# HGRN decays grown in place by doubling blocks, in a two-layer FoX/HGRN2 trunk on one core

## The chip, the cores and the metric

The kernel runs on one core of a Trainium2 chip. TensorE (PE) multiplies matrices into the PSUM banks, VectorE (DVE) and ScalarE (ACT) work element by element, GpSimd (POOL) does a few small things, and SyncE (SP) issues nearly all loads. The metric is device time in microseconds (us), the median of the runs.

## The reference, cut to what matters

The model has two layers, each with a SwiGLU half-step, a mixer and another SwiGLU half-step, over 256 positions of 1024 channels. The mixer of the first layer is an attention (FoX); that of the second, at about 70% of the span, is HGRN2, and the change lies there:

```
f = lb + (1.0 - lb) * jax.nn.sigmoid(proj[..., D:2 * D])
k = 1.0 - f
# per head (8 of them, 128 channels each), with G the running sum of log f over positions:
A[t, s] = sum over channels of  q[t] * k[s] * exp(G[t] - G[s])      for s <= t
o[t]    = sum over s of  A[t, s] * v[s]
```

exp(G[t] - G[s]) is the product of f over the positions s+1 to t. The kernel never forms it for each pair. It splits the pairs by levels: for the block size b = 64, 32, ..., 1 the pairs whose s lies in the left half and t in the right half of the same stretch of 2b positions. With the middle m of that stretch the decay is (product from s+1 to m) times (product from m to t), so that one matrix product of a decayed k and a decayed q gives a level.

## The kernel before

**Stream.** All products with weights are done as three matmuls (`mm3`, lines 745 to 747; for v in `v_token`, lines 896 to 898), on weights that come by DMA into 8 `raw` tiles and are split by ACT (`wh`, a cast, line 385) and DVE (`wl`, line 386) into a high and a low part, two blocks of weights ahead (`SPLIT_AHEAD`; `wh` and `wl` have three buffers each). Each `mm3` is a tick. Side work is written as Python generators that are advanced after so many ticks (`HG_LAG`), so that its instructions stand between those of the stream; the tile framework then fixes the order on each engine. Every engine works through its own order, one instruction after the other.

**The HGRN stage.** `hgrn` runs the blocks hgf (4, giving f and kk = 1 - f), then hgq, hgv and hgg in the order of `HG_ORDER`, then hgo, the output projection. Each half block of hgq gives the q of one head and starts its generator `hgrn_head`; up to three run at once, and of one E buffer (two exist, for even and odd heads) a head waits until the head two before it is through with its levels. ACT takes Ln of all f at once after the last Sigmoid (line 1093).

**A head.** (1) PE turns log f of its 256 positions (`plf`, line 1128, two transposes), and ACT and DVE split it into two parts (`lt`, lines 1130 and 1131). (2) PE multiplies it with a constant matrix `tmat` of prefix sums, four matmuls of 512 columns (line 1140) and four of 256 (line 1146) into the bank `pd`, which gives the log decays of the levels. (3) ACT takes Exp of them (lines 1141 and 1148; line 1150 copies f by Exp as well), and DVE multiplies them on k and q (lines 1154 to 1176). (4) PE makes `pc`, the products of the diagonal (line 1182) and of the two halves of the sequence (line 1184), and `pA`, those of the seven levels (line 1192); DVE puts them in place in `at` (line 1195, copy under a mask). (5) PE multiplies `at` by v (`pho`, lines 1203 to 1205), ACT and POOL normalise it, and PE turns it back (`hpr`, line 1218). The products of (4) and (5) are on fp32, of which the trace shows two passes for each matmul.

**Constants.** `tmat` is loaded by POOL in two parts (`tm`, lines 616 and 619) at about 64 us; the attention uses 128 of its columns.

Of the kernel before, what the change touches and what calls it, by code (L numbers as in the profile page):

```python
# [11 lines left out]
F32 = mybir.dt.float32  # L12
F32R = mybir.dt.float32r
# [6 lines left out]
P = 128  # L20
# [11 lines left out]
TM = (len(LEV) - 1) * P  # L32
# [10 lines left out]
HG_LAG = (4, 7, 14, 12, 12)  # L43
# [16 lines left out]
def shape_constants():  # L60
# [4 lines left out]
    rcross = (i[:, None] >= i[None, :]).astype(np.float32)  # L65
    tl, tr = [], []
    masks = np.zeros((P, len(LEV), P), np.int32)
    for li, b in enumerate(LEV):
        T = np.zeros((P, P), np.float32)
        for t in range(P):  # L70
            g0 = t // (2 * b) * (2 * b)
            mid = g0 + b
            if t >= mid:
                T[mid:t + 1, t] = 1
            else:
                T[t + 1:mid, t] = 1
# [13 lines left out]
    tmat = np.concatenate([lcross] + tl[:-2] + [rcross] + tr[:-2], axis=1)  # L90
    return (np.ascontiguousarray(consts), np.ascontiguousarray(tmat),
# [15 lines left out]
class Trunk:  # L107
# [29 lines left out]
    # ------------------------------------------------- interleaving of side work  # L137
# [44 lines left out]
    # ---------------------------------------------------------------- stream  # L182
# [235 lines left out]
    # ------------------------------------------------------------------- ada  # L418
# [89 lines left out]
    # ----------------------------------------------------------------- setup  # L508
    def setup(self):
# [41 lines left out]
        self.tm = cp.tile([P, TM], F32R, name="tm")  # L551
# [64 lines left out]
        nc.gpsimd.dma_start(self.tm, a["tmat"][:, :TM])  # L616
        tm1 = self.wk.tile([P, D], F32R, tag="wide", name="tm1", bufs=1)
        nc.vector.tensor_copy(tm1[:, 0:1], self.hbuf[0][:, KC - 1, 0:1])
        nc.gpsimd.dma_start(tm1[:, :TM], a["tmat"][:, TM:])
        self.hg_tm = [self.tm, tm1]  # L620
# [44 lines left out]
    # ------------------------------------------------------------------ norm  # L665
# [74 lines left out]
    # -------------------------------------------------------------- products  # L740
# [101 lines left out]
    # ------------------------------------------------------------------- ffn  # L842
# [64 lines left out]
    # ------------------------------------------------------------------- fox  # L907
    def fox(self, n):
# [53 lines left out]
        def cum_tail():  # L962
            yield CUM_LAG[0]
            pz = self.bank("zt")
            nc.tensor.transpose(pz[:, :M], z[:M, P:], self.ident[:M, :M])
            zt = self.w("zt")
            nc.scalar.copy(zt[:, :M], pz[:, :M])
            yield CUM_LAG[1]
            pz = self.bank("cum")
            nc.tensor.matmul(pz[:M, :P], zt[:, :M], self.tm[:, :P].bitcast(F32), start=True, stop=True)  # L970
            nc.vector.scalar_tensor_tensor(cum[:M, P:], pz[:M, :P], cum[:M, P - 1:P], z[:M, P:], ALU.add, ALU.add)
# [85 lines left out]
    # ------------------------------------------------------------------ hgrn  # L1057
    def hgrn(self, n):
# [10 lines left out]
        parts = [reg(4)[:, :D], reg(4)[:, D:]]  # L1069
        parts += [big[:, 10240:], wk.tile([P, D], F32, tag="adaacc", name="E_adaacc", bufs=1)]  # L1070
        parts = [t.rearrange("p (l c) -> p l c", c=P) for t in parts]
        self.hE = [parts[:2], parts[2:]]
        ox = self.ubuf
        self.hspare = wk.tile([P, S], F32, tag="adatr", name="hspare", bufs=1).rearrange("p (i c) -> p i c", i=2)

        def use_f(b, ps, sw=None):
            for c in range(2):
                h = 2 * b + c
                pc = ps[c]
                if sw is None:  # L1080
                    sg = nc.scalar.activation(f[:, h, :], pc, AF.Sigmoid)
                else:
                    sg = nc.scalar.activation(f[:, h, :], pc, AF.Sigmoid, bias=sw[:, c:c + 1])
                self.last_sig = sg.ins
# [38 lines left out]
    def hgrn_head(self, h, qs, kk, lf, v):  # L1123
        nc, wk = self.nc, self.wk
        q, k = qs[:, h, :], kk[:, h, :]
        pt = self.bank("plf")
        for t in range(2):
            nc.tensor.transpose(pt[:, t * P:(t + 1) * P], lf[:, h, t * P:(t + 1) * P], self.ident)
        lt = wk.tile([P, 512], F32R, tag="mx", name="lt", bufs=6).rearrange("p (j s) -> p j s", j=2)
        nc.scalar.copy(lt[:, 0], pt[:, :S])  # L1130
        nc.vector.tensor_tensor(lt[:, 1], pt[:, :S], lt[:, 0].bitcast(F32), ALU.subtract)
        yield HG_LAG[0]
        while h >= 2 and h - 2 not in self.e_done:
            yield E_POLL
        E = self.hE[h % 2]
        E0, E1 = E
        for t in range(2):
            pd = self.bank("pd")
            for j in range(2):
                nc.tensor.matmul(pd, lt[:, j, t * P:(t + 1) * P], self.hg_tm[t][:, :512], start=(j == 0), stop=(j == 1))  # L1140
            nc.scalar.activation(E0[:, t::2], pd.rearrange("p (l c) -> p l c", c=P), AF.Exp)
            yield HG_LAG[1]
        pd = self.bank("pd")
        for t in range(2):
            for j in range(2):
                nc.tensor.matmul(pd[:, t * S:(t + 1) * S], lt[:, j, t * P:(t + 1) * P], self.hg_tm[t][:, 512:TM],
                                 start=(t == 0 and j == 0), stop=(j == 1), skip_group_check=True)
        nc.scalar.activation(E1[:, :4].rearrange("p (l t) c -> p t l c", t=2),
                             pd.rearrange("p (t l c) -> p t l c", t=2, c=P), AF.Exp)
        nc.scalar.activation(E1[:, 4:8:2], lf[:, h, :].rearrange("p (t c) -> p t c", t=2), AF.Exp)  # L1150
        yield HG_LAG[1]
        lev = [E0[:, 2 * li:2 * li + 2] for li in range(1, 4)] + [E1[:, 2 * li:2 * li + 2] for li in range(4)]
        lev = [x.rearrange("p t c -> p (t c)") for x in lev]
        nc.vector.tensor_tensor(E0[:, 0, :], E0[:, 0, :], k[:, :P], ALU.mult)
        nc.vector.tensor_tensor(E0[:, 1, :], E0[:, 1, :], q[:, P:], ALU.mult)
        free = self.hspare[:, h % 2, :]
        ab = []
        for x, b in zip(lev[:-2], LEV):
            nc.vector.tensor_tensor(pick(free, *pair(b, b)), pick(x, *pair(b, P)), pick(k, *pair(b, P + b)), ALU.mult)
            nc.vector.tensor_tensor(pick(x[:, P:], *pair(b, b)), pick(x[:, b:], *pair(b, P)),  # L1160
                                    pick(q[:, b:], *pair(b, P - b)), ALU.mult)
            ab.append((free, x[:, P:]))
            free = x[:, :P]
# [129 lines left out]
```

## Time and profile before

| | us |
|---|---|
| median of 3 runs (1119.0 to 1120.95) | 1120.65 |
| span of the profiled execution | 1119.9 |
| PE busy | 1095.8 |
| DVE busy | 847.6 |
| ACT busy | 590.3 |
| POOL busy | 24.0 |

A busy PE is not a PE at its peak, since matmuls overlap; what a matmul costs the engine is the time to the next one, and it is read from the chain of waits. The HGRN stage with its heads lies between 793 and 903 us.

### The profile page before, as it was taken

To read this page: it belongs to the slowest core of one execution; us is meant where nothing else is said; L and a number is where in the kernel's file an instruction comes from. 1 tells how busy PE (TensorE), PEld (TensorE's weight loads), DVE (VectorE), ACT (ScalarE), POOL (GpSimd) and SP (SyncE) were. 2 spreads that over 40 slices of the span, in tenths; PEclk is the share of its full clock that TensorE was granted. 3 is DMA by queue.
4 is the path that set the end of the run, shared out by engine and by line. 5 is a ranking of instruction groups with operands and counts; after the bars stand their busy time and mean duration, and the time that the engine had idled before them with its cause. 6 is when DMAs were issued, how large, how long until landed. Compare 5 with 4: busy or idle time off the path is not lost.

```text
span 1119.9 us, 22226 instructions
## 1 busy us (share of the span) xinstructions
PE 1095.8 (98%) x8915; PEld 1066.5 (95%) x8915; DVE 847.6 (76%) x1519; ACT 590.3 (53%) x1041; POOL 24.0 (2%) x47
## 2 busy tenths in 40 slices
PE   5999999999999999999999999999999999999997
PEld 5999999988989999999999999999899999999997
DVE  6988778577995997788689888768878979555542
ACT  5464444476864754444454444346776656444443
POOL 0000000010000000000000000000000000000000
PEclk8999999999999999999999999999999999999999
DMA  9999999659783599999759999985634247665530
GB/s 287 336 336 327 327 316 289 193 192 330 249 272 102 151 278 304 308 319 320 209 175 298 295 320 338 298 250 171 186 126 136 81 133 200 190 183 172 177 110 38
DMA packets 304852, 260.97 MB, mean 233 GB/s; under 512 B 9541, under 2 KB 281389, under 8 KB 304749
## 3 DMA queue, kind: packets, MB, share of 16 engines
q1 hardware_dynamic: 304172, 257.79, 76.3%
q8 instruction: 70, 1.15, 0.4%
q0 software_dynamic: 432, 1.25, 0.3%
q10 hardware_dynamic: 144, 0.52, 0.1%
q14 instruction: 34, 0.27, 0.1%
HBM read 258.47 MB, written 1.05 MB: 232 GB/s over the span
## 4 chain that ended last, share of the span: by engine, by line
PE 77%; issue 18%; ACT 2%; DMA 1%; POOL 1%; SPq 0%; DVE 0%; POOLq 0%; DVEq 0%; ACTq 0%
PE pf L746 17%; PE pf L745 17%; PE pf L747 16%; PE pd L745 6%; PE pd L746 6%; PE pd L747 6%; PE pA L1192 1%; PE pv L898 1%; PE pv L897 1%; PE pv L896 1%; PE adaps L479 1%; PE sc L1015 1%; PE pd L1140 1%; DMA raw<-in_ffn_w_up_dram 1%; ACT wh L385 1%
## 5 line engine op out<-in xcount | busy, mean ns | idle before, releaser
L746 PE MATMUL pf<-hbuf,wh 128*128 128x256 f32 (+1 forms) x1920 | 542.4, 284 | 0.9 <-DVE hbuf L602 0.9
L747 PE MATMUL pf<-hbuf,wl 128*128 128x256 f32 (+1 forms) x1920 | 541.5, 283 | 0.0
L745 PE MATMUL pf<-hbuf,wh 128*128 128x256 f32 (+1 forms) x1920 | 538.1, 284 | 0.6 <-ACT hbuf L601 0.6
L385 ACT CAST wh<-raw 128x1024 fp32r<-128x1024 f32 x338 | 341.2, 1027 | 372.1 <-PE pf L746 207.8
L386 DVE TENSOR_TENSOR wl<-raw,wh 128x1024 fp32r<-128x1024 f32 x338 | 400.2, 1195 | 158.9 <-ACT wh L385 157.7
L745 PEld LDWEIGHTS pf<-hbuf,wh 128*128 128x128 f32 x1920 | 362.7, 191 | 5.1 <-issue 4.0
L746 PEld LDWEIGHTS pf<-hbuf,wh 128*128 128x128 f32 x1920 | 363.7, 189 | 1.4 <-DVE hbuf L602 1.1
L747 PEld LDWEIGHTS pf<-hbuf,wl 128*128 128x128 f32 x1920 | 363.3, 189 | 0.8 <-issue 0.8
L745 PE MATMUL pd<-gx,wh 128*128 128x256 f32 x704 | 198.4, 282 | 0.0
L746 PE MATMUL pd<-gx,wh 128*128 128x256 f32 x704 | 197.4, 280 | 0.0
L747 PE MATMUL pd<-gx,wl 128*128 128x256 f32 x704 | 197.4, 280 | 0.0
L426 DVE SCALAR_TENSOR_TENSOR adaacc<-raw,cond,adaacc 128x1024 f32<-128x1024 f32 x112 | 143.0, 1277 | 0.6
L745 PEld LDWEIGHTS pd<-gx,wh 128*128 128x128 f32 x704 | 132.6, 188 | 2.5 <-issue 2.5
L746 PEld LDWEIGHTS pd<-gx,wh 128*128 128x128 f32 x704 | 132.6, 188 | 0.0
L747 PEld LDWEIGHTS pd<-gx,wl 128*128 128x128 f32 x704 | 132.6, 188 | 0.0
L811 ACT CAST gx<-g 128x256 fp32r<-128x256 f32 x88 | 35.6, 406 | 25.9 <-DVE g L853 17.6
L813 DVE TENSOR_TENSOR gx<-g,gx 128x256 fp32r<-128x256 f32 x88 | 36.8, 420 | 0.3
L424 DVE TENSOR_SCALAR adaacc<-raw,cond 128x1024 f32<-128x1024 f32 x16 | 12.1, 756 | 25.2 <-PE adaps L479 25.2
L853 DVE TENSOR_TENSOR g<-sa,pf 128x256 f32<-128x256 f32 x73 | 30.1, 415 | 0.6 <-ACT sa L852 0.2
L818 DVE SCALAR_TENSOR_TENSOR x<-pd,mod,x 128x256 f32<-128x256 f32 x32 | 14.3, 480 | 21.1 <-PE pd L747 21.1
L852 ACT ACTIVATE sa<-pf 128x256 f32<-128x256 f32 x73 | 27.4, 377 | 0.0
L374 ACT CAST wh<-raw 128x896 fp32r<-128x896 f32 x16 | 15.0, 936 | 23.0 <-DMA raw<-in_ffn_w_up_dram 23.0
(246 smaller groups left out, 894.9 us busy)
## 6 DMA issues: line engine op xcount, KB each, us to landing
raw<-in_ffn_w_up_dram SPq DMA_DIRECT2D x162, 512.0 KB, 5.8
raw<-in_ada_w_dram SPq DMA_DIRECT2D x128, 512.0 KB, 6.1
raw<-in_ffn_w_down_dram SPq DMA_DIRECT2D x76, 512.0 KB, 5.5
raw<-in_fox_w_in_dram SPq DMA_DIRECT2D x32, 512.0 KB, 4.9
raw<-in_hgrn_w_in_dram SPq DMA_DIRECT2D x32, 512.0 KB, 4.6
raw<-in_ada_w_dram SPq DMA_DIRECT2D x32, 256.0 KB, 6.5
raw<-in_ffn_w_up_dram SPq DMA_DIRECT2D x16, 448.0 KB, 6.3
raw<-in_fox_w_out_dram SPq DMA_DIRECT2D x8, 512.0 KB, 5.7
```

The source lines that it names most:

```text
L374: nc.scalar.copy(wh[:, k, cs], raw)
L385: nc.scalar.copy(wh[:, ks, cs], raw)
L386: nc.vector.tensor_tensor(wl[:, ks, cs], raw, wh[:, ks, cs].bitcast(F32), ALU.subtract)
L426: nc.vector.scalar_tensor_tensor(self.ada_acc, raw, self.cond[:, k:k + 1], self.ada_acc, ALU.mult, ALU.add)
L745: nc.tensor.matmul(ps, wh, hx[:, :n], start=first, stop=False, skip_group_check=True)
L746: nc.tensor.matmul(ps, wh, hx[:, lo:lo + n], start=False, stop=False, skip_group_check=True)
L747: nc.tensor.matmul(ps, wl, hx[:, :n], start=False, stop=last, skip_group_check=True)
L811: nc.scalar.copy(dst[:, :S], v)
L813: nc.vector.tensor_tensor(dst[:, lo:lo + S], v, dst[:, :S].bitcast(F32), ALU.subtract)
L818: nc.vector.scalar_tensor_tensor(self.x[:, m, :], ps, gate[:, m:m + 1], self.x[:, m, :], ALU.mult, ALU.add)
L852: nc.scalar.activation(sa, ps[0], AF.Silu)
L853: nc.vector.tensor_tensor(g, sa, ps[1], ALU.mult)
```

## The change

The logarithm, the prefix sums, the Exp and the transposes go. The decays are products of f that grow with b. Before the levels, `totals` multiplies neighbouring f for all heads at once: `tot2` holds the products of pairs, `tot4` of fours, and `tots` those of 8, 16, 32 and 64. In a head q is first multiplied by f. Then at each level, b = 1 first, ACT copies the left halves of k and the right halves of q into two packed slots (`snap`), the operands of that level's product; after that DVE multiplies in place those parts of q and k that lie beyond the next middle by the total of their neighbour block (`grow`), and b doubles. The levels 1 to 8 are multiplied in one bank, 16 to 64 in a second, with the product of the two halves, which has left `pc`. The E buffers become slots; `tmat` shrinks from 1536 to 128 columns; `HG_LAG` changes.

```diff
-HG_LAG = (4, 7, 14, 12, 12)
+HG_LAG = (4, 4, 5, 12, 12)
...
-        nc.gpsimd.dma_start(self.tm, a["tmat"][:, :TM])
-        nc.gpsimd.dma_start(tm1[:, :TM], a["tmat"][:, TM:])
+        nc.gpsimd.dma_start(self.tm, a["tmat"])
...
-        with self.tc.issue_after(self.last_sig):
-            for b in range(2):
-                nc.scalar.activation(f[:, 4 * b:4 * b + 4, :], f[:, 4 * b:4 * b + 4, :], AF.Ln)
+        self.totals(f)
...
+    def totals(self, f):
+        halve = lambda o, x: nc.vector.tensor_tensor(o, x[:, 0::2], x[:, 1::2], ALU.mult)
+        halve(self.tot2, flat)
+        for i in range(2):
+            halve(self.tot4[i], self.tot2[:, i * 512:(i + 1) * 512])
+            halve(self.tots[:, i * P:(i + 1) * P], self.tot4[i])
+        for n in (256, 128, 64):
+            halve(self.tots[:, o + n:o + n + n // 2], self.tots[:, o:o + n])
+
+    def grow(self, x, t, b, left):
+        m = P // b
+        if left:
+            v, w = pick(x, *pair(b, P + b)), pick(t[:, 1:], [m - 1, 2], [2, m // 2], [0, b])
+        else:
+            v, w = pick(x[:, b:], *pair(b, P - b)), pick(t, [m + 1, 2], [2, m // 2], [0, b])
+        self.nc.vector.tensor_tensor(v, v, w, ALU.mult)
...
-        for t in range(2):
-            nc.tensor.transpose(pt[:, t * P:(t + 1) * P], lf[:, h, t * P:(t + 1) * P], self.ident)
-        nc.scalar.copy(lt[:, 0], pt[:, :S])
-        nc.vector.tensor_tensor(lt[:, 1], pt[:, :S], lt[:, 0].bitcast(F32), ALU.subtract)
...
-                nc.tensor.matmul(pd, lt[:, j, t * P:(t + 1) * P], self.hg_tm[t][:, :512], start=(j == 0), stop=(j == 1))
-            nc.scalar.activation(E0[:, t::2], pd.rearrange("p (l c) -> p l c", c=P), AF.Exp)
...
+        nc.vector.tensor_tensor(q, q, f[:, h, :], ALU.mult)
+        def snap(i):
+            b = ups[i]
+            nc.scalar.copy(pick(slots[2 * i], *pair(b, b)), pick(k, *pair(b, P + b)))
+            nc.scalar.copy(pick(slots[2 * i + 1], *pair(b, b)), pick(q[:, b:], *pair(b, P - b)))
...
+        snap(0)
+        for i, b in enumerate(ups):
+            yield HG_LAG[1]
+            t = self.total(h, f, b)
+            if i < len(ups) - 1:
+                self.grow(q, t, b, False)
+                self.grow(k, t, b, True)
+                snap(i + 1)
+            else:
+                nc.vector.tensor_scalar(q[:, P:P + b], q[:, P:P + b], t[:, 3:4], None, ALU.mult)
+                nc.vector.tensor_scalar(k[:, :b], k[:, :b], t[:, 1:2], None, ALU.mult)
+            if i == 4:
+                level(0, 4, False)
+        yield HG_LAG[2]
+        level(4, 7, True)
```

On PE, where the first block of v (hgv) begins and the heads 0 and 1 run side by side, before (L896 to L898 are the stream; `tm_854` is the second part of `tmat`):

```order
L896 MATMUL pv_9744<-wh_9612,hbuf_117 128x512
L897 MATMUL pv_9744<-wl_9613,hbuf_117 128x512
L898 MATMUL pv_9744<-wh_9612,hbuf_117 128x512
L1140 MATMUL pd<-tm_854,lt 128x512 x4
L896 MATMUL pv_9743<-wh_9612,hbuf_117 128x512
```

The same block now, at the levels 1 to 8 of both heads, which stand 39 stream matmuls and the four of `pc` behind the start of hgv:

```order
L881 MATMUL pv_9747<-wh_9690,hbuf_118 128x512
L1162 MATMUL pA<-hgbig 128x128 x8
L879 MATMUL pv_9748<-wh_9690,hbuf_118 128x512
L880 MATMUL pv_9748<-wl_9691,hbuf_118 128x512
L881 MATMUL pv_9748<-wh_9690,hbuf_118 128x512
```

What stood between the stream's matmuls for the decays is gone, and the level products stand there earlier.

On ACT, in the same block, before (L385 is the cast of weights):

```order
L1150 ACTIVATE hgbig<-hgbig 128x2x128
L1150 ACTIVATE E_adaacc<-hgbig 128x2x128
L1141 ACTIVATE hgbig<-pd 128x4x128 x4
L385 CAST wh_9810<-raw_0_9548 128x1024
L385 CAST wh_9810<-raw_1_9614 128x1024
L1148 ACTIVATE hgbig<-pd 128x2x2x128
```

Now (L371 is that cast; L1155 copies k, L1156 q, and the innermost number is b):

```order
L371 CAST wh_9820<-raw_1_9612 128x1024
L1155 COPY hgbig<-hgbig 128x2x4x16
L1156 COPY hgbig<-hgbig 128x2x4x16
L1155 COPY E_adaacc<-hgbig 128x2x4x16
L1156 COPY E_adaacc<-hgbig 128x2x4x16
L1155 COPY hgbig<-hgbig 128x2x64 x2
```

Few large instructions on PSUM have become many small ones on SBUF, with the casts among them.

On DVE, in the same block, now (L1134 is `grow`, two heads with q and k each, L372 the split of weights, L1169 the copy under a mask):

```order
L1134 TENSOR_TENSOR hgbig<-hgbig 128x2x64 x4
L1134 TENSOR_TENSOR hgbig<-hgbig,tot_9336 128x2x32x2 x4
L1134 TENSOR_TENSOR hgbig<-hgbig 128x2x16x4 x4
L372 TENSOR_TENSOR wl_9821<-raw_0_9546,wh_9820 128x1024
L1134 TENSOR_TENSOR hgbig<-hgbig,tots 128x2x8x8 x4
L372 TENSOR_TENSOR wl_9821<-raw_1_9612,wh_9820 128x1024
L1134 TENSOR_TENSOR hgbig<-hgbig,tots 128x2x4x16 x2
L1169 COPY_PREDICATED at<-lmask,pA 128x2x64
```

Each group of four waits for ACT's copies of the level before, and those copies wait for the group before it. In the whole program PE has 80 matmuls fewer than before and none more, ACT 7 loads of its function tables where it had 13, and 112 copies more.

## Rows read from the trace of the kernel before

**Rows 1.** The page's first lines: span, and busy time of each engine with its share and instructions.
```profile
span 1119.9 us, 22226 instructions
...
PE 1095.8 (98%) x8915; PEld 1066.5 (95%) x8915; DVE 847.6 (76%) x1519; ACT 590.3 (53%) x1041; POOL 24.0 (2%) x47
```

**Rows 2.** The view by stretches: the stage of the heads, and the stretch of the first half-step in which `tmat` is loaded. Columns: stretch, its length, busy us and instructions of PE, PEld (weight loads), DVE, ACT, POOL, the granted clock, the DMA share, GB/s.
```profile
793.00:903.00 110.00, 108.75 (x797) 101.50 (x796) 90.14 (x287) 70.62 (x161) 5.95 (x8) 1.00 0.40 123
...
30.00:140.00 110.00, 109.14 (x922) 107.84 (x922) 93.80 (x164) 53.62 (x86) 1.64 (x3) 1.00 1.13 331
```

**Rows 3.** The chain of waits in order of time, pieces of PE: start, us, what, and how many records follow one another.
```profile
793.65 0.44 PE plf L1128 x4
...
798.69 0.93 PE pd L1140 x4
...
802.40 0.94 PE pd L1146 x8
...
810.37 0.44 PE pc L1182 x4
...
811.03 1.56 PE pA L1192 x14
...
817.91 0.23 PE pv L896
...
842.04 0.12 PE pf L745
```

**Rows 4.** Groups of PE's instructions from 793 to 903 us: the three that the change removes, with their counts (busy us, mean ns of one, idle time before).
```profile
L1140 PE MATMUL pd<-tm,lt 128*128 128x512 f32 x32 | 10.6, 412 | 0.0
...
L1146 PE MATMUL pd<-tm,lt 128*128 128x256 f32 x32 | 5.0, 284 | 0.0
...
L1128 PE MATMUL plf<-ident,hgbig 128*128 128x128 f32 x16 | 2.9, 272 | 0.0
```

**Rows 5.** Groups of DVE's instructions in the same stretch: the weight split, the copy under a mask, and one of the products of decays.
```profile
L386 DVE TENSOR_TENSOR wl<-raw,wh 128x1024 fp32r<-128x1024 f32 x24 | 29.1, 1221 | 6.9 <-ACT wh L385 6.9
L1195 DVE COPY_PREDICATED at<-lmask,pA 128x128 f32<-128x128 int32 x56 | 18.1, 341 | 0.9 <-PE pA L1192 0.4
L1160 DVE TENSOR_TENSOR hgbig<-hgbig 128x128 f32<-128x128 f32 x32 | 9.1, 291 | 0.7
```

**Rows 6.** DVE in order of time: start, us (of the whole row), what, how many in a row.
```profile
791.07 1.21 DVE L386 TENSOR_TENSOR wl<-raw,wh 128x1024 fp32r<-128x1024 f32 x1
...
799.57 0.22 DVE L1172 TENSOR_TENSOR hgbig<-hgbig 128x32 f32<-128x32 f32 x1
799.70 0.21 DVE L1173 TENSOR_TENSOR hgbig<-hgbig 128x32 f32<-128x32 f32 x1
...
805.10 0.49 DVE L1159 TENSOR_TENSOR hgbig<-hgbig 128x128 f32<-128x128 f32 x2
...
813.91 2.36 DVE L1195 COPY_PREDICATED at<-lmask,pA 128x128 f32<-128x128 int32 x10
```

**Rows 7.** The stretch 793 to 903 us of ACT alone: first all that reads `pd` (columns PE, PEld, DVE, ACT, clock, DMA), then all on line 1150 (column ACT, its table loads among them).
```profile
793.00:903.00 110.00, 15.60 (x64) 10.00 (x64) 0.00 (x0) 14.09 (x24) 1.00 0.40 123
...
793.00:903.00 110.00, 5.83 (x10) 1.00 0.40 123
```

**Rows 8.** Groups of ACT's instructions in the same stretch: the cast of `lt`, the two table loads of line 1150, and the copy of 128 columns from PSUM.
```profile
L1130 ACT CAST lt<-plf 128x256 fp32r<-128x256 f32 x8 | 3.0, 384 | 0.0
...
L1150 ACT ACT_TABLE_LOAD x2 | 2.6, 1283 | 2.7 <-PE pA L1192 2.7
...
L1187 ACT COPY at<-pc 128x128 f32<-128x128 f32 x8 | 2.0, 268 | 0.0
```

**Rows 9.** ACT and DVE in order of time: how soon an instruction follows on its own engine (the first two), and on another one (the last two; in brackets the idle time before it and who ended it).
```profile
839.10 0.27 ACT L1187 COPY at<-pc 128x128 f32<-128x128 f32 x1
839.26 0.42 ACT L1150 ACTIVATE hgbig<-hgbig 128x256 f32<-128x256 f32 x1
...
784.31 0.15 DVE L786 COPY sw<-pf 128x1 f32<-128x1 f32 x1
...
784.49 0.91 ACT L1083 ACTIVATE hgbig<-fold,sw 128x256 f32<-128x256 f32 x2 [0.77 <-DVE sw L786]
```

**Rows 10.** Who waited for whom from 776 to 932 us: total us, times, longest.
```profile
ACT wh L385 <- PE pf L746: 10.3, 6, 2.9
...
DVE wl L386 <- ACT wh L385: 6.9, 6, 2.6
...
PE hpr L1218 <- ACT hon L1214: 1.2, 2, 0.7
...
PEld pd L1140 <- DVE lt L1131: 0.3, 1, 0.3
PEld pd L1140 <- ACT lt L1130: 0.2, 1, 0.2
```

**Rows 11.** The chain of waits of a late head, from the product with v to the transpose back: start, us, what.
```profile
889.00 0.64 ACT hon L1209 x4
...
891.13 0.59 PE hpr L1218 x2
```

**Rows 12.** The DMA issues from 0 to 120 us, those of `tmat`: how many, KB each, median us to landing.
```profile
tm<-in_tmat_dram POOLq DMA_DIRECT2D x2, 384.0 KB, 7.4
```

More of the change, by code (lines that the diff above doesn't have):

```diff
@@ L550, in setup @@
         nc.gpsimd.memset(self.mhalf, -0.5)
-        self.tm = cp.tile([P, TM], F32R, name="tm")
+        self.tm = cp.tile([P, P], F32R, name="tm")
+        self.tots = cp.tile([P, 480], F32, name="tots")
         self.identb = cp.tile([P, P], BF16, name="identb")
@@ L1068, in hgrn @@
         q = reg(3).rearrange("p (k c) -> p k c", c=S)
[L1069 to L1072, printed above, removed]
+        tail = wk.tile([P, D], F32, tag="adaacc", name="E_adaacc", bufs=1)
+        slots = [reg(4)[:, i * P:(i + 1) * P] for i in range(16)]
+        slots += [t[:, i * P:(i + 1) * P] for t in (big[:, 10240:], tail) for i in range(8)]
+        self.snaps = [slots[:14], slots[16:30]]
+        self.tot2 = wk.tile([P, D], F32, tag="wide", name="tot2", bufs=1)
+        self.tot4 = [reg(4)[:, 14 * P:], tail[:, 6 * P:]]
         ox = self.ubuf
-        self.hspare = wk.tile([P, S], F32, tag="adatr", name="hspare", bufs=1).rearrange("p (i c) -> p i c", i=2)
         def use_f(b, ps, sw=None):
@@ new lines, in total @@
+    def total(self, h, f, b):
+        if b == 1:
+            return f[:, h, :]
+        n = S // b
+        if b == 2:
+            return self.tot2[:, h * n:(h + 1) * n]
+        if b == 4:
+            return self.tot4[h // 4][:, h % 4 * n:(h % 4 + 1) * n]
+        o = {8: 0, 16: 256, 32: 384, 64: 448}[b] + h * n
+        return self.tots[:, o:o + n]
+    def grow(self, x, t, b, left):
[5 more added lines that the diff above has]
+        self.nc.vector.tensor_tensor(v, v, w, ALU.mult)
@@ L1144, in hgrn_head @@
[L1144 to L1163, printed above, removed]
@@ L1171, in hgrn_head @@
[L1171 to L1179 removed]
+        slots = self.snaps[h % 2]
@@ L1183, in hgrn_head @@
                              start=(t == 0), stop=True, skip_group_check=True)
[L1184 removed]
+        yield HG_LAG[0]
+        at = wk.tile([P, 512], F32, tag="mx", name="at", bufs=6)
         for t in range(2):
             nc.vector.tensor_tensor(at[:, t * P:(t + 1) * P], self.ident, pc[:, t * P:(t + 1) * P], ALU.mult)
[L1187 to L1196 removed]
+        nc.vector.tensor_tensor(q, q, f[:, h, :], ALU.mult)
@@ new lines, in hgrn_head, with level @@
+        ups = LEV[::-1]
+        def snap(i):
+            b = ups[i]
+            nc.scalar.copy(pick(slots[2 * i], *pair(b, b)), pick(k, *pair(b, P + b)))
+            nc.scalar.copy(pick(slots[2 * i + 1], *pair(b, b)), pick(q[:, b:], *pair(b, P - b)))
+        def level(l0, l1, cross):
+            pa = self.bank("pA")
+            for i in range(l0, l1):
+                o = (i - l0) * P
+                nc.tensor.matmul(pa[:, o:o + P], slots[2 * i], slots[2 * i + 1], start=(o == 0), stop=True,
+                                 skip_group_check=True)
+            if cross:
+                nc.tensor.matmul(pa[:, 3 * P:], k[:, :P], q[:, P:], start=False, stop=True, skip_group_check=True)
+                nc.scalar.copy(at[:, S:S + P], pa[:, 3 * P:])
+            for i in range(l0, l1):
+                b = ups[i]
+                nc.vector.copy_predicated(pick(at[:, b:], *pair(b, P - b)),
+                                          pick(self.lmask[:, LEV.index(b), :], *pair(b, b)),
+                                          pick(pa[:, (i - l0) * P:], *pair(b, b)))
```

68 lines of the change are left out of this document (9 added, 59 removed).

## The prediction

> **What bounds the kernel now.** I read the page's head first: PE is busy for 1095.8 of 1119.9 us [rows 1]. A busy PE need not be at its limit, so the stage that the change touches comes next. [...] The chain of waits is the third view. There PE's matmuls follow one another at their own pace: three stream matmuls of 256 columns take 3 x 0.12 us, one of 512 takes 0.23, and the decay products run at the same pace (four of 512 in 0.93, eight of 256 in 0.94) [rows 3]. Nothing stands between them. The waits of PE in the stage are small: 1.2 us for `hon` ahead of `hpr`, and 0.3 and 0.2 us of its weight loads for `lt` [rows 10]. So the stage lasts as long as PE's work, and what is taken from PE is gained, as long as DVE and ACT still deliver in time. They are no idle helpers: DVE has 20 us left in 110, ACT 39.
>
> **What the change takes from PE.** A head loses two transposes, four matmuls of 512 columns and four of 256: over eight heads 16, 32 and 32 [rows 4]. At the pace of the chain [rows 3]: 16 x 0.44/4 = 1.76 us; 32 x 0.93/4 = 7.44 us; 32 x 0.94/8 = 3.76 us. Sum 12.96, say 13.0 us. Busy times and means of the groups would give more (412 ns for one of 512), but they overlap and are not the cost. The product of the two halves only moves from one bank to another. All of this lies on the path that sets the end. The waits of the weight loads for `lt` go too, 0.5 us [rows 10].
>
> **DVE.** A head loses 20 instructions (one of 256 columns, 13 of 128, six small ones) and gets 15 (`q` times `f` with 256, twelve `grow` of 128, two scalings of 64). One alone takes 0.29 us [rows 5], in a run two take 0.49, so each further one 0.20 [rows 6]; the small ones follow after 0.13 [rows 6]; one of 256 takes 0.42 alone, worked out from 0.29 for 128 and 1.22 for 1024 [rows 5], and 0.33 in a run. Removed: 13 x 0.20 + 0.33 + 6 x 0.15 = 3.8 us; added: 12 x 0.20 + 0.33 + 2 x 0.13 = 3.0 us. Over eight heads that is 6 us less. `totals` adds eight instructions once: 1.2 us for 1024 products (as L386), two of 256, four of 128 and smaller, 3.1 us in sum. So DVE has some 87 us of work, in a stage of 97 us instead of 110: 90% where it was 82%. No row shows a product with a repeated (stride 0) operand. Rows of blocks and of plain 128 columns take the same 0.29 [rows 5], so I take 0.20 to 0.29, nearest to the rows, and leave 0.5 to a rival.
>
> **ACT.** In the stage it loses 14.1 us on `pd` and 5.8 us on line 1150 with its two table loads [rows 7], 3.0 us of `lt` and two more loads at 1.28 us [rows 8], 25 us in all. It gets 112 copies of 128 columns. The nearest row is the copy from PSUM, 0.27 us [rows 8], behind which the next instruction starts after 0.16 [rows 9]; from SBUF I take 0.32 alone and 0.21 in a run (an instruction on 256 SBUF columns takes 0.42 [rows 9], less 128 x 0.83 ns). That is 18 to 36 us: ACT stays between 63 and 82 of 97 us. It is not the bound by sum.
> [...]
>
> **The new chain, and where PE must wait for it.** Before, ACT and DVE met once in a head; now they hand each level to each other, seven times. A hand-over costs little: DVE's copy ends at 784.46 and ACT starts at 784.49 [rows 9]. For one head a level is 0.29 + 0.32 + 0.05 = 0.66 us, for two heads side by side four chains at 0.20 to 0.21, 0.84 us. The lags give a level four ticks of 0.36 us, 1.43 us, plus the matmuls of the heads themselves. So the chain fits, unless casts and splits get between its links, and they do: the order shows them there.
> I walk the first pair, which has no slack ahead of it. PE begins hgv at 792.96 (three matmuls before 793.65 [rows 3]) and comes to the level products behind 39 x 0.23 + 0.9 us of `pc`, at 802.9. DVE is through with f at 791.07 [rows 6]. Then come `tot2` (1.2), a split (1.15), four more totals (1.1), and two splits whose casts need the weight buffer that hgq's end frees at 793, and between which ACT copies q: the second cast ends at 795.7, its split at 796.8. `at`, the last totals and q times f take 1.8 us, to 798.6, and the first copy of q lands at 798.9. Three levels take 2.5 us, to 801.4; a cast (1.05) stands ahead of ACT's next four copies (0.84), so the slots of the levels 1 to 8 are full at 803.3. PE waits 0.4 us. The second place is 27 matmuls further (9 x 0.23 + 18 x 0.12, and 1.8 us of `pA`), with the product of the halves at about 809.9. DVE needs two splits, three groups of `grow`, eight masked copies at 0.23 [rows 6] and the scalings, which I make 810 to 811. So the first pair costs PE 1.0 us (0 to 3).
> The other six heads start one by one, so that each meets less work of a twin; I take 0.25 us each, 1.5 us (0 to 4.5). At the end the transpose back stands 12 `mm3` matmuls or 1.4 us behind the product with v, where the chain over Square, POOL and the scaling took 2.1 us [rows 11]; before, decay products of a later head partly filled such a gap. That is 0.7 us for each of three heads, 2.1 where 1.2 was [rows 10]: 0.9 us more (0 to 2).
>
> **Hidden parts.** Loading `tmat` moves 2 x 384 KB [rows 12]; nearly all of it goes, but PE is busy for 109.1 of 110 us there [rows 2], so I count nothing; if a late load were behind the 0.9 us that is left, that much would be gained at most. The Ln and the table loads are on ACT, which had time.
>
> **Sum.** -13.0 - 0.5 + 1.0 + 1.5 + 0.9 = -10.1 us. The profiled execution has a span of 1119.9 us, the median of the runs is 1120.65, and I take the same 0.75 us around the span: 1110.5 us. The bounds are 13.5 + 1.2 us (all waits gone), 1106, and waits of 9.5 us, 1116.6.
>
> **Rivals.**
> (B) The in-order queues stretch the levels. ACT's cast waits for a weight buffer that PE frees (10.3 us in six waits), and DVE's split for the cast (6.9 us) [rows 10], and the next level queues behind both. A level with one cast and one split shared by two levels in series costs 0.84 + 0.5 x (1.06 + 1.22) = 2.0 us. In each of four generations of heads seven levels then take 14 us, against 7 x 4 + 5 ticks or 11.8 us and some 1.5 us of `pA`, `pc` and `pho` that stand in them: 0.7 us each, and 1 to 2 us more where a cast waits for PE. That is 7 to 11 us of waits, and of the 13.5 us a gain of 3 to 7 is left: 1114 to 1118. For it speaks that the order has casts between the links; against it that PE's positions in the order leave slack of 0.6 us a level.
> [...]
> (C) DVE becomes the bound. If the repeated operand makes a `grow` cost 0.35 us instead of 0.20, 96 of them add 14 us; DVE then needs 101 us, more than PE's 97, and with its own waits the stage lasts the old 110: no change, 1118.4 to 1122.9.
> (D) Slower: the hand-over chain itself sets the stage. It must eat the 13.5 us and 2.2 us more, 15.7 us over four generations, 3.9 us each: a level must cost (13.3 + 3.9)/7 = 2.5 us or more, three times the 0.84 of the rows. That needs both a cast and a split in series at each level (0.84 + 1.06 + 1.22 = 3.1 us). At 2.7 us the waits are 4 x (18.9 - 13.3) = 22 us and the kernel is 9 us slower, at 3.1 us it is 20: 1130 to 1141. Against it: 24 splits stand against 56 levels [rows 5].
> That the change does not do what it says is excluded by the order, which has the 80 matmuls fewer.
>
> **How the numbers follow.** Forecast (gain of 7 to 14 us) 0.68; B 0.17; C 0.07; D 0.08. Faster by over 0.2% (2.2 us, about what a measurement of this kernel can tell from no change) is the forecast and B: 0.85; within 0.2% C: 0.07; slower D: 0.08. The range from 1106.5 to 1117.5 holds the forecast and nearly all of B, some 0.83.
>
> **What would show it right or wrong.** Right: the chain of waits in the stage still made of PE's pieces, the groups of lines 1128, 1140 and 1146 gone, and hgv to the last `hpr` some 10 us shorter. The walk is right if PE's waits name `pA` and the product of the halves at the first pair, by 0 to 3 us. B and D would show as idle time of PE ahead of `pA` in each head, ended by ACT's copies, with ACT's copies waiting for DVE; C as DVE busy without gaps and `grow` at over 0.35 us. Wrong altogether would be a stage that is as long as before with no PE wait in it: then the removed matmuls had cost nothing.

## The result and the profile after

The kernel after takes 1108.42 us (median of 4 runs, 1106.51 to 1109.91), the kernel before 1120.39 in runs taken beside it (1119.0 to 1120.95). The ratio is 0.9891, 95% interval 0.9879 to 0.9902: faster by 1.1%, or 12.0 us, where 10.1 were forecast; 1108.42 lies inside the forecast range. A second measurement of the same kernel gave 1108.79 us and 0.9894 (0.9879 to 0.9909).

The page's head answers to [rows 1]:

```profile
span 1107.3 us, 22063 instructions
...
PE 1081.0 (98%) x8835; PEld 1052.2 (95%) x8835; DVE 839.8 (76%) x1486; ACT 588.4 (53%) x1105; POOL 24.3 (2%) x46
```

PE's busy time falls by 14.8 us, the span by 12.6. DVE is busy for 7.8 us less in sum and ACT for 1.9, which speaks for a gain on PE; the run `pe_back` below shows it. How much of it lies in the HGRN stage is read between two marks that both kernels have, in PE's order of time: the `rb` of the norm ahead of the mixer and the first `nps` of the norm behind it. Before:

```profile
768.10 0.68 PE L705 MATMUL rb<-diag,ones 128*128 128x128 f32 x4 [0.32 <-DVE diag L704]
...
922.32 0.50 PE L692 MATMUL nps<-ones,sqacc 128*128 128x1 f32 x4
```

After:

```profile
766.44 0.68 PE L688 MATMUL rb<-diag,ones 128*128 128x128 f32 x4 [0.32 <-DVE diag L687]
...
910.81 0.50 PE L675 MATMUL nps<-ones,sqacc 128*128 128x1 f32 x4
```

That is 154.22 us before and 144.37 after: the stage gave 9.85 us. The mark at its start comes 1.66 us earlier already. That by itself says little: over all profiled runs it stands anywhere from 764.13 us (lag2) to 769.26 (tmat_back). What is gained outside of the stage is the subject of the run `after_pad` below.

Who waited for whom from 776 to 920 us, answering to [rows 10] (total us, times, longest; `hgbig` holds q, k and slots, `hon` is the normalised output of a head):

```profile
DVE wl L372 <- ACT wh L371: 8.0, 8, 1.6
ACT hgbig L1156 <- DVE hgbig L1150: 5.2, 3, 2.5
PEld hpr L1208 <- ACT hon L1204: 4.5, 4, 1.6
...
PE hpr L1208 <- ACT hon L1204: 3.7, 4, 1.4
...
DVE hgbig L1134 <- ACT hgbig L1156: 3.4, 10, 1.4
...
PEld pc L1144 <- ACT hgbig L1079: 0.9, 3, 0.4
```

The list holds no wait of PE for `pA` and none for the product of the halves. ACT and DVE do wait for each other, level by level, but PE isn't there yet when they do. PE waits in one place, ahead of the transpose back `hpr`: 3.7 us in four heads where it was 1.2 in two.

The levels of the first pair, DVE in order of time:

```profile
796.60 0.42 DVE L1150 TENSOR_TENSOR hgbig<-hgbig 128x256 f32<-128x256 f32 x1
796.93 0.89 DVE L1134 TENSOR_TENSOR hgbig<-hgbig 128x128 f32<-128x128 f32 x4
797.74 0.90 DVE L1134 TENSOR_TENSOR hgbig<-hgbig,tot 128x128 f32<-128x128 f32 x4
798.55 0.90 DVE L1134 TENSOR_TENSOR hgbig<-hgbig 128x128 f32<-128x128 f32 x4
799.97 1.23 DVE L372 TENSOR_TENSOR wl<-raw,wh 128x1024 fp32r<-128x1024 f32 x1 [0.52 <-ACT wh L371]
801.11 0.89 DVE L1134 TENSOR_TENSOR hgbig<-hgbig,tots 128x128 f32<-128x128 f32 x4
...
807.28 0.25 DVE L1182 TENSOR_SCALAR hgbig<-hgbig,tots 128x64 f32<-128x64 f32 x1
```

PE in the same stretch:

```profile
801.27 1.95 PE L1162 MATMUL pA<-hgbig 128*128 128x128 f32 x16
807.31 0.83 PE L1162 MATMUL pA<-hgbig 128*128 128x128 f32 x6
807.98 0.39 PE L1165 MATMUL pA<-hgbig 128*128 128x128 f32 x2
```

A level of two heads takes 0.81 us (796.93, 797.74, 798.55), until a cast on ACT and its split on DVE stand between (799.97). The last copy that the first bank needs starts on ACT at 800.43 and lasts 0.30; PE comes at 801.27, 0.5 us later. The last scaling of k and q ends at 807.53, and the product of the halves stands at 807.98. PE waits in neither place; the operands are there about half a microsecond before.

What the new instructions cost, groups of DVE and of ACT from 793 to 893 us (busy us, mean ns of one, idle time before and its releasers):

```profile
L1134 DVE TENSOR_TENSOR hgbig<-hgbig,tots 128x128 f32<-128x128 f32 x48 | 13.0, 292 | 2.6 <-ACT hgbig L1155 1.8 <-ACT hgbig L1156 0.5 <-ACT E_adaacc L1156 0.2
```

```profile
L1156 ACT COPY hgbig<-hgbig 128x128 f32<-128x128 f32 x44 | 13.1, 303 | 9.0 <-DVE hgbig L1150 5.2 <-DVE hgbig L1134 3.8
```

The repeated operand of `grow` costs nothing extra here: 292 ns, where the plain product of [rows 5] takes 291. Four in a row take 0.89 us, so each further one 0.20.

The chain of waits at the last head answers to [rows 11]:

```profile
888.39 0.24 PE pho L1195 x2
888.65 0.64 ACT hon L1199 x4
889.63 0.70 POOL hms L1202
890.35 0.38 ACT hon L1204
890.77 0.33 PE hpr L1208
```

From the first Square (888.65) to the transpose it is 2.1 us, as before the change.

### The profile page after: what moved, and what is told of

It reads as the page before. It is cut to its first block, busy times and chain, and to the rows that moved or that the text cites. A ratio compares the mean times of both kernels' runs of the same rounds, so it can differ in the third digit from the quotient of the medians.

```text
span 1107.3 us, 22063 instructions
## 1 busy us (share of the span) xinstructions
PE 1081.0 (98%) x8835; PEld 1052.2 (95%) x8835; DVE 839.8 (76%) x1486; ACT 588.4 (53%) x1105; POOL 24.3 (2%) x46
## 4 chain that ended last, share of the span: by engine, by line
PE 73%; issue 18%; ACT 3%; DVE 2%; POOL 1%; DMA 1%; SPq 1%; POOLq 0%; DVEq 0%; ACTq 0%
PE pf L728 16%; PE pf L729 16%; PE pf L730 16%; PE pd L728 6%; PE pd L729 6%; PE pd L730 6%; ACT wh L371 1%; PE pv L881 1%; PE pv L879 1%; PE pv L880 1%; PE adaps L465 1%; PE sc L998 1%; DVE wl L372 1%; DMA raw<-in_ffn_w_up_dram 1%; PE pA L1162 1%
## 5 line engine op out<-in xcount | busy, mean ns | idle before, releaser
L371 ACT CAST wh<-raw 128x1024 fp32r<-128x1024 f32 x338 | 341.5, 1027 | 367.5 <-PE pf L729 211.0
L372 DVE TENSOR_TENSOR wl<-raw,wh 128x1024 fp32r<-128x1024 f32 x338 | 399.9, 1194 | 157.8 <-ACT wh L371 156.8
```

The lines of the kernel that those rows point to most:

```text
L371: nc.scalar.copy(wh[:, ks, cs], raw)
L372: nc.vector.tensor_tensor(wl[:, ks, cs], raw, wh[:, ks, cs].bitcast(F32), ALU.subtract)
```

## The experiments

My theory: the stage lasts as long as PE's work, the gain is the pace of 80 matmuls that left PE (the time from the start of one to the start of the next), less what PE now waits ahead of `hpr`. The rival: ACT and DVE were relieved (Exp, table loads, `lt`), and that is the gain. Further questions: what slack the growth chain has, where the gain outside of the stage comes from, and what the tail costs.

The length of the stage, between the marks `rb` and `nps` above, and the waits of PE ahead of `hpr` and of `pA`, from each run's trace. The kernel before was run anew beside each group of runs (medians 1120.39, 1120.76, 1121.57 and 1121.01 us), and each ratio is to those:

| kernel | us (median) | ratio, 95% interval | stage, us | `hpr`, us | `pA`, us |
|---|---|---|---|---|---|
| before | 1120.39 | | 154.22 | 1.2 | 0 |
| after | 1108.42 | 0.9891 (0.9879 to 0.9902) | 144.37 | 3.7 | 0 |
| pe_back | 1118.36 | 0.9975 (0.9963 to 0.9986) | 154.72 | 1.6 | 0 |
| half_prefix | 1114.68 | 0.9945 (0.9932 to 0.9958) | 148.53 | 1.3 | 0 |
| no_exp | 1121.01 | 0.9996 (0.9987 to 1.0006) | 153.93 | 1.2 | 0 |
| snap2 | 1110.35 | 0.9907 (0.9895 to 0.9919) | 147.25 | 2.7 | 0.6 |
| after_pad | 1110.48 | 0.9911 (0.9897 to 0.9926) | 144.29 | 3.7 | 0 |
| lag3 | 1105.89 | 0.9866 (0.9850 to 0.9881) | 141.84 | 0.9 | 0.4 |
| lag3s4 | 1107.84 | 0.9876 (0.9860 to 0.9892) | 143.20 | 0.8 | 0.3 |
| lag2 | 1105.96 | 0.9865 (0.9850 to 0.9880) | 142.14 | 0.7 | 1.1 |
| after_again | 1108.79 | 0.9894 (0.9879 to 0.9909) | 144.35 | 3.7 | 0 |
| lag2s4 | 1106.09 | 0.9870 (0.9854 to 0.9886) | 142.02 | 0.4 | 0.9 |
| tmat_back | 1108.46 | 0.9903 (0.9886 to 0.9919) | 144.32 | 3.7 | 0 |

The length of the stage repeats within 0.1 us where the stage is the same (after, after_pad, after_again, tmat_back), far better than the whole time, of which the part ahead of the stage moves by up to 5 us from one profiled run to another. The granted clock of TensorE has a share in that: from 228.6 to 231.6 us it is 0.50 in before and after, and stream matmuls of 258 columns follow one another there after 0.21 us, where at 1.00 they follow after 0.12. Over the whole of the profiled execution the mean is 0.992 in before and 0.999 in no_exp, whose stage begins 3.3 us earlier (764.82 against 768.10). In the stage of before and after it is 1.00. So small effects are read from the stage. One length in the table needs a correction: in snap2 eight stream matmuls more, 0.96 us, stand ahead of `nps`, where all other runs have the same stream matmuls between the marks.

### Is it PE? pe_back, half_prefix, no_exp

**pe_back**, the kernel after with the matmuls put back, unread:

```diff
+        pt = self.bank("plf")
+        for t in range(2):
+            nc.tensor.transpose(pt[:, t * P:(t + 1) * P], k[:, t * P:(t + 1) * P], self.ident)
         pc = self.bank("pc")
...
             yield HG_LAG[1]
+            if i < 3:
+                pd, n = self.bank("pd"), 512 if i < 2 else S
+                for j in range(2 if i < 2 else 4):
+                    o = n * (j // 2) % 512
+                    nc.tensor.matmul(pd[:, o:o + n], self.tm[:, :P], self.h[:, j, :n], start=(j == 0), stop=True,
+                                     skip_group_check=True)
```

> The kernel after, with PE matmuls of the kind that the change removed put back and nothing read from them: per head two transposes ahead of pc, two of 512 columns after level 1, two of 512 after level 2 and four of 256 after level 4 (80 in all). ACT and DVE do what they do after the change. Theory (the gain is PE's own pace): they cost 13.0 us again, less what of them now fills the 4.4 us in which PE waits for the late heads: 1118 to 1121.4 us, so no gain over the kernel before is left. Rival (the gain came from ACT and DVE, which lost the Exp, the table loads and lt, and PE had room): 1107 to 1110, as the kernel after.

1118.36 us: of the 12.0 us some 2 are left (2.4 against the kernel before run beside it), about what is gained outside of the stage (see after_pad). In the stage the matmuls cost 10.35 us (154.72 against 144.37), while the wait ahead of `hpr` falls from 3.7 to 1.6 us; both together make 12.5 us of the 13.0 that they were priced at. The stage is then as long as before the change, though ACT and DVE work in the new way. The rival is out, and so is the thought that the new lags are the gain: pe_back keeps them.

**half_prefix**, the kernel before with half of the prefix sums:

```diff
-            for j in range(2):
-                nc.tensor.matmul(pd, lt[:, j, t * P:(t + 1) * P], self.hg_tm[t][:, :512], start=(j == 0), stop=(j == 1))
+            nc.tensor.matmul(pd, lt[:, 0, t * P:(t + 1) * P], self.hg_tm[t][:, :512], start=True, stop=True)
...
-            for j in range(2):
-                nc.tensor.matmul(pd[:, t * S:(t + 1) * S], lt[:, j, t * P:(t + 1) * P], self.hg_tm[t][:, 512:TM],
-                                 start=(t == 0 and j == 0), stop=(j == 1), skip_group_check=True)
+            nc.tensor.matmul(pd[:, t * S:(t + 1) * S], lt[:, 0, t * P:(t + 1) * P], self.hg_tm[t][:, 512:TM],
+                             start=(t == 0), stop=True, skip_group_check=True)
```

> The kernel before, without the low part of the log decays in the prefix sums (half of lines 1140 and 1146, 16 matmuls of 512 columns and 16 of 256, are left out, so the decays are less exact); ACT and DVE do all that they did. Theory: 16 x 0.2325 + 16 x 0.1175 = 5.6 us less, 1114.8, or a little less gain where these matmuls covered a wait for a late head: 1114.5 to 1116. Rival (PE's time was not the cost): 1119.5 to 1121.

1114.68 us, and the stage is 5.69 us shorter, where the chain's pace had given 5.6. Half of the busy time of these two groups in [rows 4] would be 7.8 us. So the price of these matmuls was their pace in the chain of waits, not their busy time.

**no_exp**, the kernel before:

```diff
-                nc.scalar.activation(f[:, 4 * b:4 * b + 4, :], f[:, 4 * b:4 * b + 4, :], AF.Ln)
+                nc.scalar.activation(f[:, 4 * b:4 * b + 4, :], f[:, 4 * b:4 * b + 4, :], AF.Copy)
...
-            nc.scalar.activation(E0[:, t::2], pd.rearrange("p (l c) -> p l c", c=P), AF.Exp)
+            nc.scalar.activation(E0[:, t::2], pd.rearrange("p (l c) -> p l c", c=P), AF.Copy)
```

(and so at the two other Exp)

> The kernel before with Ln and Exp in the HGRN mixer replaced by plain copies (so the decays are left out: what is computed with is not the decay), which removes the loads of ACT's function tables there and nothing else; PE and DVE are as before. Theory (PE paces the stage): no change, 1119.5 to 1121.5, at most the few tenths that PE waited for lt. Rival (ACT's relief is the gain, six table loads of 1.28 us): 1113 to 1117.

1121.01 us, 0.9996 (0.9987 to 1.0006); the stage is 0.3 us shorter. Six table loads fewer on ACT are worth next to nothing here.

### What slack has the chain? snap2, lag2

**snap2**, the kernel after, in `snap`:

```diff
             nc.scalar.copy(pick(slots[2 * i + 1], *pair(b, b)), pick(q[:, b:], *pair(b, P - b)))
+            nc.scalar.copy(pick(slots[2 * i], *pair(b, b)), pick(k, *pair(b, P + b)))
+            nc.scalar.copy(pick(slots[2 * i + 1], *pair(b, b)), pick(q[:, b:], *pair(b, P - b)))
```

> The kernel after with every packed copy on ACT done twice: 112 copies more, at 0.20 us in a run 22 us and at 0.30 us alone 34 us, in a stage of 98 us in which ACT is now busy for 70.7 us of 100. A level of two heads side by side then costs 8 x 0.21 = 1.7 us where the lags leave 1.43 us, one head alone 0.29 + 0.32 + 2 x 0.2 + 0.05 = 1.1 us. Theory (the hand-over chain has slack that is used up only now): the first pair waits for pA by 0.5 to 3 us, the single heads little: 1109 to 1113. Rival (the copies are on the path already): the whole 22 us and more, over 1125. Third case (ACT has that room and the chain too): 1107 to 1110.

1110.35 us; the stage is 2.9 us longer between the marks and 1.9 without the eight matmuls said above, as the medians have it too (1110.35 against 1108.42). This is for 112 copies that add 18 us to ACT's busy time from 793 to 893 us:

```profile
793.00:893.00 100.00, 98.17 (x731) 92.02 (x730) 82.14 (x250) 88.88 (x328) 5.62 (x7) 1.00 0.43 133
```

After (the fourth of the pairs is ACT):

```profile
793.00:893.00 100.00, 96.34 (x724) 90.69 (x723) 81.41 (x251) 70.73 (x224) 6.75 (x8) 1.00 0.44 132
```

The size was as the theory had it, the place wasn't: the first pair did not wait. The longest wait is ahead of the last `hpr` (1.9 us), and the levels of later heads add 0.6 us ahead of `pA` and 0.4 ahead of `pho`. The wait ahead of `hpr` is shorter in sum (2.7 us against 3.7), so these waits account for little of the 1.9 us; where the rest goes was not taken apart. PE's order changed with the copies as well: the 16 records of `pA` for the first pair, one row in after, stand in three rows with stream matmuls between (PE in order of time):

```profile
802.04 1.50 PE L1164 MATMUL pA<-hgbig 128*128 128x128 f32 x12
...
803.84 0.38 PE L1164 MATMUL pA<-hgbig 128*128 128x128 f32 x2
...
804.75 0.39 PE L1164 MATMUL pA<-hgbig 128*128 128x128 f32 x2
```

So chain and order together have slack for most of another 18 us of ACT; this run doesn't say how much of it is the chain's alone.

**lag2**, the kernel after:

```diff
-HG_LAG = (4, 4, 5, 12, 12)
+HG_LAG = (4, 2, 5, 12, 12)
```

> The kernel after with a lag of 2 ticks at the levels, 0.72 us where the chain of a pair takes 0.81 and that of one head 0.66, without the casts and splits that stand between. Theory (PE waits as soon as the lag is under the chain): every head waits for pA, 0.5 to 1.5 us each: 1109 to 1115. Rival (matmuls of the other heads and the stream's own order leave enough room): 1105 to 1108.5.

My expectation missed: 1105.96 us, faster, the rival's case. PE waited for `pA` twice only, in single heads between blocks of 256 columns (PE in order of time; in brackets the idle time and who ended it):

```profile
861.17 0.49 PE L1162 MATMUL pA<-hgbig 128*128 128x128 f32 x2 [0.59 <-ACT hgbig L1156]
...
871.37 0.49 PE L1162 MATMUL pA<-hgbig 128*128 128x128 f32 x2 [0.49 <-ACT hgbig L1156]
```

I had priced every tick at 0.36 us, three matmuls of 256 columns. In the blocks of v a tick is three of 512 columns, 0.69 us (3 x 0.23, [rows 3]), and levels of the heads 0 to 3 lie there: even two ticks give a level 1.4 us. The same error stands in the prediction where it says what the lags leave to a level. It doesn't cover the heads 4 to 7, whose levels stand between blocks of 256 columns: there the two waits of 1.1 us in sum are all that half the lag cost, less than the 0.5 to 1.5 us for each head that I expected.

### The tail: lag3, lag3s4, lag2s4

**lag3**, the kernel after:

```diff
-HG_LAG = (4, 4, 5, 12, 12)
+HG_LAG = (4, 3, 4, 12, 12)
```

> The kernel after with lags of 3 and 4 ticks in place of 4 and 5 at the levels and ahead of the second bank. Theory (the growth chain has slack, the lost time is the tail): a level of two heads has 1.07 us for the 0.81 us that it takes, PE waits for pA by 0 to 1.5 us, and heads start up to 2 us earlier but the last one's transpose still stands 1.4 us behind its product with v: 1106 to 1109.5. Rival (the lag of 4 is needed, since casts and splits stand between the links): PE waits ahead of pA by 4 us and more: over 1112.

**lag3s4**, that and, at `SIDE`, up to four heads at once:

```diff
-SIDE = (3, 3)
+SIDE = (3, 4)
```

> As lag3, and up to four heads at once, so that the heads go in pairs and the last transposes stand 3.5 us behind the product with v, with stream matmuls between. Theory (the 3.7 us that PE waits ahead of hpr after the change come from late heads with nothing between): these waits go to under 1 us and nothing comes in their place but 0 to 2 us ahead of pA: 1105 to 1108.5. Rival (four chains on DVE and ACT at once take it back at pA, 4 x 7 levels of pairs): 1108.5 to 1113.

**lag2s4**, the same with shorter lags:

```diff
-HG_LAG = (4, 4, 5, 12, 12)
+HG_LAG = (4, 2, 3, 12, 12)
-SIDE = (3, 3)
+SIDE = (3, 4)
```

> The kernel after with a lag of 2 ticks at the levels, 3 ahead of the second bank, and up to four heads at once: the last transposes stand 4 us of stream matmuls behind their product with v, the last product of levels 2 us ahead of it. Theory (what is left of waits is the transpose of the last head, 0.9 us in lag2, and 2 us ahead of pA where levels meet casts): the waits ahead of hpr fall under 0.3 us, those of pA stay between 1 and 3 us: 1104.5 to 1107. Rival (two heads at each level and half the lag put PE behind ACT's copies in all four generations): over 1108.5.

In all of them the wait ahead of `hpr` falls from 3.7 us to between 0.4 and 0.9. lag3 comes out 0.1 us under its range, and its stage is 2.5 us shorter than that of after; that of lag2s4 is 2.35 shorter, with 0.4 us ahead of `hpr`, a little more than expected, and 0.9 ahead of `pA`, a little less. In lag3s4 the stage gains 1.2 us only: the `pc` of a new pair waits 1.2 us for ACT's copy of q, which stands behind a cast, a wait that my expectation did not have. The theory holds for the waits ahead of `hpr`, and pairs of heads are no better than heads that start sooner. By their medians lag3, lag2 and lag2s4 are all faster than the kernel after (1105.9 to 1106.1 us, against 1108.4 and 1108.8 in its two measurements), and their stages are 2.2 to 2.5 us shorter; the intervals of their ratios just touch those of after, and I take none of the three as the best.

**after_again** is the kernel after, run beside lag2s4 and tmat_back.

> The kernel after, unchanged, beside the next two on one chip: 1107 to 1110, 0.989 of the kernel before. All theories agree; it measures the comparison of the versions.

### The gain outside the stage: after_pad, tmat_back

**after_pad**, the kernel after with an unused buffer of 640 bytes in each partition, the difference between the old `tm` and the new `tm` and `tots`:

```diff
         self.tots = cp.tile([P, 480], F32, name="tots")
+        pad = cp.tile([P, 160], F32, name="pad")
+        nc.gpsimd.memset(pad[:, 0:1], 0.0)
```

> The kernel after with an unused buffer of 160 columns behind the totals, which puts all buffers that are laid out later (weights, work buffers) back at the places that they have in the kernel before; nothing else is changed. The question is the 2.3 us that the kernel after gains outside the HGRN stage, in the four down-projections of the half-steps, where neither kernel waits. Theory (the places of the buffers set the pace there: in the kernels before, half_prefix and no_exp the down-projection from 505 to 560 us takes 119 ns a matmul, in after, pe_back and snap2 117.5): the pace goes back to 119, 1110 to 1112. Rival (it is run scatter, or comes with something else of the change): as after, 1107 to 1110, and the pace stays at 117.5.

1110.48 us. The stretch between two products of `adaps` in the third down-projection shows it, on PE in order of time. In the kernel before:

```profile
504.56 0.64 PE L479 MATMUL adaps<-adaacc,ones 128*32 128x256 f32 x8
537.36 0.64 PE L479 MATMUL adaps<-adaacc,ones 128*32 128x256 f32 x8
```

After:

```profile
504.13 0.64 PE L465 MATMUL adaps<-adaacc,ones 128*32 128x256 f32 x8
536.39 0.64 PE L465 MATMUL adaps<-adaacc,ones 128*32 128x256 f32 x8
```

after_pad:

```profile
502.40 0.64 PE L465 MATMUL adaps<-adaacc,ones 128*32 128x256 f32 x8
535.20 0.64 PE L465 MATMUL adaps<-adaacc,ones 128*32 128x256 f32 x8
```

32.80, 32.26 and again 32.80 us, for the same matmuls, without a wait of PE in any of them and, from 505 to 569 us, at a granted clock of 1.00 in all three. With the buffers back at their old places the old pace is back to the hundredth. From 569 us to the stage, and from its end to the end of the program, after_pad keeps step with before, within 0.01 us in the first stretch and 0.1 in the second, while after gains 0.43 us in the first and, up to the last `nps`, 0.75 in the second. With 0.66 us from 135 to 228 us and 0.79 from 505 to 569 that is 2.6 us in the four half-steps; the medians of after_pad and after differ by 2.1 (by 1.7 with after_again). That the places of the buffers set this is shown; which buffer meets which is not, and was not tried.

**tmat_back**, the kernel after with two loads of 384 KB put back:

```diff
-        nc.gpsimd.dma_start(self.tm, a["tmat"])
+        nc.gpsimd.dma_start(self.tm, a["tmat"][:, :P])
+        tm1 = self.wk.tile([P, D], F32R, tag="wide", name="tm1", bufs=1)
+        nc.vector.tensor_copy(tm1[:, 0:1], self.hbuf[0][:, KC - 1, 0:1])
+        nc.gpsimd.dma_start(tm1[:, :6 * P], a["tmat"][:, :6 * P])
+        nc.gpsimd.dma_start(tm1[:, :6 * P], a["tmat"][:, 6 * P:])
```

> The kernel after with the loads of the large constant put back (two of 384 KB by POOL into the buffer that tm1 had, nothing reads them; the buffer is written anew later). Theory (the load is hidden): as after, 1107 to 1110. Rival (the load held back the first half-step by the 0.9 us that PE is not busy there): up to 0.9 us more than after_again.

1108.46 us, as after_again (1108.79). The medians alone could hide a few tenths, but the traces of before, which has such loads, and of after, which has not, agree: PE's wait nearest to them is 0.86 us at 61.77 us in before and 0.86 at 62.14 in after, both times for `hbuf`, which DVE writes, and from 62 to 68 us the granted clock is 1.00 in both. Behind it, with the loads under way, PE is busy for all 36.00 us from 64 to 100 us in before. So the load was hidden.

## Why the prediction was right, step by step

- **PE sets the stage, and a matmul costs its pace in the chain: right.** 13.0 us were forecast; putting the matmuls back showed 12.45 with the waits that they fill, and half_prefix 5.69 of 5.6. The stage as a whole gave 9.85 us where the sum had 10.1. What DVE and ACT had left in the stage, 20 and 39 us, comes from their busy times in [rows 2].
- **Waits for `lt`, 0.5 us: gone from the list, but no gain of that size shows.** pe_back has no `lt` and the 80 matmuls, and its stage is 0.5 us longer than that of before, of which 0.4 us are its longer wait ahead of `hpr`.
- **First pair, 1.0 us (0 to 3): none.** The walk came close. Moved by the 1.66 us by which the stage begins earlier, PE came to `pA` at 802.9, as forecast, and the slots were full at 802.4 instead of 803.3; at the product of the halves it was 809.6 against 809.2, not 809.9 against 810 to 811. I had put the cast ahead of the copies behind DVE's third group; it ran beside it (798.89 against 798.55). The casts and splits that I had counted up to the second place were there, and it kept the 0.9 us. The level of 0.84 us was right (0.81).
- **Six other heads, 1.5 us (0 to 4.5): none ahead of `pA`.** The tick explains it for two of them: a level in a block of v has 2.8 us and not 1.43. The heads 4 to 7 have the 1.43 us (their `pA` stand from 847.6 us on, between matmuls of 256 columns) and did not wait either; the 0.25 us for each had no row behind it.
- **Tail, 0.9 us (0 to 2): 2.5.** The term that came out of its bounds. I took 2.1 us for the chain, as in [rows 11], and three heads. Four heads wait, and two links were longer. `hms` on DVE stands behind its other work: at the first of the four, ACT is through with Square at 864.09 and `hms` starts at 865.24, behind a split, two products and a masked copy:

```profile
863.31 1.22 DVE L372 TENSOR_TENSOR wl<-raw,wh 128x1024 fp32r<-128x1024 f32 x1
...
865.24 0.16 DVE L1201 TENSOR_SCALAR hms<-hms 128x2 f32<-128x2 f32 x1
```

And POOL's power took 0.99 us at the first, 1.63 at the second and 0.69 at the other two. POOL in order of time:

```profile
839.17 0.69 POOL L1202 TENSOR_TENSOR hms<-hms,mhalf 128x2 f32<-128x2 f32 x1 [21.01 <-DVE hms L1201]
...
871.42 1.63 POOL L1202 TENSOR_TENSOR hms<-hms,mhalf 128x2 f32<-128x2 f32 x1 [4.95 <-DVE hms L1201]
...
889.63 0.69 POOL L1202 TENSOR_TENSOR hms<-hms,mhalf 128x2 f32<-128x2 f32 x1 [8.66 <-DVE hms L1201]
```

DVE at these three times:

```profile
839.47 0.42 DVE L1150 TENSOR_TENSOR hgbig<-hgbig 128x256 f32<-128x256 f32 x1
...
871.28 1.23 DVE L372 TENSOR_TENSOR wl<-raw,wh 128x1024 fp32r<-128x1024 f32 x1
...
889.58 0.42 DVE L1089 SCALAR_TENSOR_TENSOR gt<-gt,pf 128x256 f32<-128x256 f32 x1
```

The one of 1.63 us runs beside a split that reads two buffers in SBUF and had started 0.14 us before it, and ends 0.63 us after the next instruction on DVE has begun (872.42); that of 0.69 at 889.63 runs beside an instruction that reads one operand from PSUM. But in the kernel before a power took 0.69 us (856.21) behind a product of two buffers in SBUF that had started 0.17 us earlier (856.04, 0.28 us), and at 839.47 such a product started 0.30 us behind a power, which took 0.69, and itself took the 0.42 us that it takes elsewhere (796.60). What makes a power long is not shown: no run here takes it apart.
- **The sum.** The terms for `pA` were 2.5 us too dear, the tail 1.6 too cheap. With what was measured for the waits the sum would be -13.0 - 0.5 + 2.5 = -11.0 us, and the stage shows 9.85: some 1.15 us are missing. pe_back divides them: 0.55 us is the price of the matmuls (12.45 in place of 13.0), and about 0.6 the gain from `lt` that doesn't show. Waits of the weight loads for `pc`, 0.9 us in three in after and none in before, may have taken that back, which no run takes apart. That the sum came within 0.3 us of the stage is luck: errors of both signs made up for each other.
- **Hidden parts: right** (tmat_back, no_exp). **Rival C is out** (`grow` 292 ns). **B and D did not come**: no wait ahead of `pA`, and snap2 has to add 18 us of ACT before 1.9 us of the stage are lost.
- **The price of a copy.** A copy takes 303 ns here; in a run they follow one another after 0.20 us, so 0.1 us of each overlaps with the next. The prediction had taken 0.32 alone and 0.21 in a run. The 0.83 ns a column in its estimate lies between what ACT shows in the stage before: 1058 ns for a cast of 1024 columns and 407 for one of 256, 0.85 ns a column, and 1043 for the Ln of 1024 and 420 for the Exp of 256, 0.81. PE never waited for a copy ahead of `pA`.
- **1108.4 instead of 1110.5.** The 2.1 us between are the places of the buffers, as far as medians tell: after_pad, with the buffers where they were, takes 1110.48. No step of mine had it, and that 1110.48 meets the forecast so closely is luck as well, by the errors above.

## What to carry to other kernels

Price a removed matmul by its pace in the chain of waits (5.6 us in half_prefix, where 5.69 came), and check by putting it back unread: the wait that it used to fill is then seen too (2.1 us ahead of `hpr` in pe_back). Count lags in the matmuls that really stand there: a tick was 0.69 us in the blocks of v and 0.36 in the others. Before lengths between two marks are compared, count what stands between them in each run (snap2). When small work leaves PE, look at the ends of the generations: here the chain over ACT, DVE and POOL ahead of `hpr` came out bare (3.7 us of waits where it was 1.2), and an earlier start of the heads covered it again (0.9 in lag3, 0.7 in lag2).

## What was not expected of the hardware

- The pace of matmuls without any wait changed here with the places of the buffers: 640 bytes in each partition moved a stretch of the down-projection from 32.80 to 32.26 us (1.6%) and back. The resized buffer moved the whole time by some 0.2% by itself (1108.42 against 1110.48 us); a pad of the old size takes that apart.
- A two-column power on POOL took 0.69 us or up to 1.63: that of 1.63 ran beside a VectorE split of 1.23 us that reads two buffers in SBUF and had started 0.14 us before. The cause is not shown.
